# A stable log-sum-exp: the first load split into two rows and fourteen

## The chip, the core and the metric

The kernel runs on one core of one Trainium2 chip. The metric is the device time of one execution in microseconds, the median of the runs shown. One further execution is recorded by the hardware profiler; all durations of single instructions and packets come from that one.

## The reference

For each of 32 x 512 rows of 1,024 float32 numbers, drawn from a normal distribution, one number is wanted:

```python
max_x = np.max(x, axis=-1, keepdims=True)
return max_x.squeeze(-1) + np.log(np.sum(np.exp(x - max_x), axis=-1))
```

That is 16,384 rows, or 67.1 MB to read and 65.5 KB to write.

## The kernel before

The kernel computes log(sum(exp(x))) without the maximum, and checks at the end that every sum lies between 1e-15 and 1e15; only if one does not, a branch computes everything again with the maximum. With these inputs the branch is not taken.

The 16,384 rows are spread over 128 partitions, 128 rows to each. The first 112 rows of each partition (`W`) are one contiguous piece of the input, the other 16 (`B`) another. Below, "a row" means one row in every partition: 128 x 4 KB, or 512 KB.

The table `LOADS` is the whole plan. Each entry is one DMA: its size in rows, and what is done with the rows that it completes. Loads shrink from 16 rows to less than one. All are issued by SP, in the order of the table, on one queue (`load`, line 127). Each has its own semaphore (`landed[i]`), and ACT waits for it (`act.wait(landed[i], 16)`).

All loads go into `ring`, a buffer of 48 rows in each partition. The first 48 rows fill it once; a later load has to wait until the reductions that read its place are done. `users` holds who last used which part, and `load` makes SP wait for every user that overlaps the new load.

ACT takes the exponential of every row in place (line 212). The row sums are then made in one of several ways, which the letter in the table names:

- `R16`: one DVE `reduce_sum` over 16 rows (line 223).
- `F9`: POOL adds the upper half of each row to the lower one (line 217), and DVE sums the halves (line 159).
- `T3`: DVE adds the halves and sums the result in one instruction for each row (line 232).
- `Y` and `Z`: the last row, in two pieces; ACT sums while it takes the exponential (line 190).

For a group of a kind, ACT issues one instruction for all its rows, and so does DVE for `R`.

The order of the work on each engine is the order in which the function emits it; no scheduler moves anything, with one exception. The first load is taken out of its place when the program is finalised, and is put on SP's list ahead of the barrier at which all engines meet at the start (`start_early`):

```python
first_load = first_load or dma.ins
...
first = here.instructions.pop(k)
...
top.insert(k, first)
```

The second and all later loads are issued behind that barrier.

At the end ACT takes the logarithm of the sums in three pieces (lines 251, 262 and 264), SP stores them with two DMAs (lines 259 and 268), and PE and DVE work out whether all sums were in range (lines 134 to 148, 274 to 283).

Of the kernel before, what the change touches and what calls it, by code (L numbers as in the profile page):

```python
# [15 lines left out]


LOADS = [
    (16, "R16"), (16, "R16"), (16, "R16"), (16, "F9 R7"), (13.5, "F6 R7"), (12.5, "R7 F6"),
    (9, "R5 F4"), (7.5, "F4 R3"), (5.5, "F4 R2"), (4.59375, "T4"), (3.25, "T3"), (2.5, "T3"),  # L20
    (1.78125, "T2"), (1.25, "T1"), (0.9375, "T1"), (0.6875, "T1"), (0.53125, "Y"), (0.46875, "Z"),
]
# [372 lines left out]
```

## Time and profile before

| What | Value |
|---|---|
| median of three runs | 162.02 us (161.79 to 163.18) |
| profiled execution | 161.82 us |
| its span, first to last instruction | 160.5 us |
| ACT busy | 114.5 us (71%) |
| DVE busy | 113.8 us (71%) |
| POOL busy | 37.2 us (23%) |
| DMA, mean over the span | 419 GB/s |
| first load issued | 0.00 us |
| second load issued | 1.44 us |
| first exponential starts | 21.92 us |
| last exponential starts | 158.02 us |

Times in the profile count from the span's start, which is the issue of the first load. "Busy" does not count time in which an instruction waits for a semaphore. In the timeline each row gives the start, the time taken, the engine, the line, the operation, output and input, the number of instructions merged into the row, and in brackets how long the engine had been idle before and what ended that. "SPq" rows are the issues of DMAs by SP, not the transfers.

### The profile page before, as it was taken

How to read it: one execution, taken by the hardware profiler on the slowest of the kernel's cores; microseconds unless marked ns; L12 is line 12 of the kernel's file. 1: busy time of each engine (PE TensorE's matmuls, PEld its weight loads, DVE VectorE, ACT ScalarE, POOL GpSimd, SP SyncE). 2: the span in 40 equal slices, each digit the busy share in tenths (PEclk: the TensorE clock that was granted, in tenths of full speed). 3: DMA queues.
4: the chain of work that ended last, by engine and by line, in shares of the span. 5: the costliest groups of instructions: out<-in, count | busy, mean ns of one | idle time of the engine just before them, and what ended most of it. 6: DMA issues, size and time to landing. Idle time of an engine off the chain costs nothing.

```text
span 160.5 us, 208 instructions
## 1 busy us (share of the span) xinstructions
PE 2.1 (1%) x24; PEld 1.0 (1%) x24; DVE 113.8 (71%) x53; ACT 114.5 (71%) x30; POOL 37.2 (23%) x10
## 2 busy tenths in 40 slices
PE   0000000000000000000000000000000000000022
PEld 0000000000000000000000000000000000000011
DVE  0000000009999499994999859959999999999995
ACT  3000059990799708995099949992999979989996
POOL 0000000000000000000000993690004969873000
DMA  8996996996996996996999999999999999999992
GB/s 278 506 523 278 506 523 261 523 523 261 523 523 261 523 506 278 523 490 294 482 441 441 441 425 408 408 408 498 423 423 404 406 426 421 449 406 427 417 407 80
DMA packets 2880, 67.18 MB, mean 419 GB/s; under 512 B 576, under 2 KB 704, under 8 KB 1344
## 3 DMA queue, kind: packets, MB, share of 16 engines
q1 hardware_dynamic: 2880, 67.18, 97.7%
HBM read 67.11 MB, written 0.07 MB: 419 GB/s over the span
## 4 chain that ended last, share of the span: by engine, by line
DMA 55%; DVE 22%; ACT 20%; SPq 0%; issue 0%; PE 0%; DVEq 0%
DMA ring<-in_x_dram 55%; ACT ring L212 20%; DVE sumexp L223 15%; DVE ring L232 4%; DVE sumexp L159 2%; SPq L127 0%; DVE clamped L139 0%; DVE clamped L134 0%; PE count L148 0%; PE count L280 0%; DVE clamped L274 0%; DVE fine L283 0%; DVEq L44 0%
## 5 line engine op out<-in xcount | busy, mean ns | idle before, releaser
L212 ACT ACTIVATE ring<-ring 128x16384 f32<-128x16384 f32 (+16 forms) x22 | 111.6, 5121 | 43.1 <-DMA ring<-in_x_dram 43.1
L223 DVE TENSOR_REDUCE sumexp<-ring 128x16 f32<-128x16384 f32 (+4 forms) x9 | 85.6, 9514 | 43.1 <-ACT ring L212 43.1
L217 POOL TENSOR_TENSOR ring<-ring 128x2048 f32<-128x2048 f32 (+2 forms) x6 | 37.0, 6171 | 108.5 <-ACT ring L212 108.5
L159 DVE TENSOR_REDUCE sumexp<-ring 128x4 f32<-128x2048 f32 (+2 forms) x6 | 18.4, 3078 | 0.1
L232 DVE SCALAR_TENSOR_TENSOR ring<-ring 128x512 f32<-128x512 f32 x15 | 9.5, 687 | 0.0
L115 ACT ACT_TABLE_LOAD x1 | 1.3, 1283 | 1.4 <-PEq L57 1.4
L144 PE MATMUL count<-far,bad 128*1 128x1 f32 x2 | 0.2, 164 | 153.3 <-DVE clamped L139 153.3
L148 PE MATMUL count<-sumexp,ones 128*1 128x1 f32 x20 | 1.8, 164 | 3.5 <-DVE ring L232 3.4
L232 DVE DVE_READ_ACCUMULATOR ring<-ring 128x1 f32 x15 | 1.2, 83 | 0.0
L190 ACT ACTIVATE last_exp<-ring 128x544 f32<-128x544 f32 (+1 forms) x2 | 1.2, 578 | 0.0
L116 DVE MEMSET ones<- 128x1 f32 x1 | 0.1, 59 | 1.5 <-PEq L57 1.5
L144 PEld LDWEIGHTS count<-far,bad 128*1 128x1 f32 x2 | 0.1, 82 | 153.3 <-DVE clamped L139 153.3
L148 PEld LDWEIGHTS count<-sumexp,ones 128*1 128x1 f32 x20 | 0.8, 81 | 4.4 <-DVE ring L232 4.3
L283 DVE TENSOR_SCALAR fine<-count 1x1 int32<-1x1 f32 x1 | 0.1, 145 | 0.5 <-PE count L148 0.5
L190 ACT ACTIVATION_READ_ACCUMULATOR last_exp<-ring 128x1 f32 x2 | 0.4, 186 | 0.0
L139 DVE SCALAR_TENSOR_TENSOR clamped<-clamped,sumexp 128x119 f32<-128x119 f32 x1 | 0.3, 283 | 0.0
L264 ACT ACTIVATE res<-sumexp 128x1 f32<-128x1 f32 x1 | 0.3, 294 | 0.0
L251 ACT ACTIVATE res<-sumexp 128x112 f32<-128x112 f32 x1 | 0.3, 280 | 0.0
L134 DVE TENSOR_SCALAR clamped<-sumexp 128x119 f32<-128x119 f32 x1 | 0.2, 223 | 0.0
L274 DVE SCALAR_TENSOR_TENSOR clamped<-sumexp 128x9 f32<-128x9 f32 x1 | 0.2, 169 | 0.1
L262 ACT ACTIVATE res<-sumexp 128x15 f32<-128x15 f32 x1 | 0.2, 198 | 0.0
L280 PE MATMUL count<-far,bad 128*1 128x1 f32 x2 | 0.2, 164 | 0.0
(8 smaller groups left out, 0.7 us busy)
## 6 DMA issues: line engine op xcount, KB each, us to landing
ring<-in_x_dram SPq DMA_DIRECT2D x1, 6912.0 KB, 23.9
ring<-in_x_dram SPq DMA_DIRECT2D x1, 6400.0 KB, 19.7
ring<-in_x_dram SPq DMA_DIRECT2D x1, 4608.0 KB, 15.9
ring<-in_x_dram SPq DMA_DIRECT2D x1, 3840.0 KB, 12.4
ring<-in_x_dram SPq DMA_DIRECT2D x1, 2816.0 KB, 18.7
ring<-in_x_dram SPq DMA_DIRECT2D x1, 2352.0 KB, 23.8
ring<-in_x_dram SPq DMA_DIRECT2D x1, 1664.0 KB, 21.1
ring<-in_x_dram SPq DMA_DIRECT2D x1, 1280.0 KB, 23.7
```

The costliest lines, as they stand in the source:

```text
L115: nc.scalar.preload_act_table_set("natural_log_exp_and_others")
L139: dve.did(nc.vector.scalar_tensor_tensor(out=clamped[:, 0:LATE], in0=clamped[:, 0:LATE], scalar=0.0, in1=sumexp[:, 0:LATE], op0=ALU.bypass ...
L144: pe.did(nc.tensor.matmul(count, lhsT=bad[:, 0:1], rhs=far, start=True, stop=False))
L148: return pe.did(nc.tensor.matmul(count, lhsT=ones, rhs=sumexp[:, c : c + 1], **kw))
L159: at = dve.did(nc.vector.reduce_sum(out=sumexp[:, c0 : c0 + s0], in_=halves, axis=AX.X))
L190: at = act.did(nc.scalar.activation(out=last_exp[:, here - p : end - p], in_=ring[:, here:end], func=AF.Exp, accum_out=sumexp[:, LAST : NC ...
L212: at = act.did(nc.scalar.activation(out=v, in_=v, func=AF.Exp))
L217: at = pool.did(nc.gpsimd.tensor_tensor(out=rows[:, :, 0:H], in0=rows[:, :, 0:H], in1=rows[:, :, H:d], op=ALU.add))
L223: who = (dve, dve.did(nc.vector.reduce_sum(out=sumexp[:, c : c + s], in_=rows, axis=AX.X)))
L232: who = (dve, dve.did(nc.vector.scalar_tensor_tensor(out=lo, in0=lo, scalar=1.0, in1=rows[:, r, H:d], op0=ALU.mult, op1=ALU.add, accum_out ...
L251: ln_early = act.did(nc.scalar.activation(out=res[:, 0:W], in_=sumexp[:, 0:W], func=AF.Ln))
L264: ln_last = act.did(nc.scalar.activation(out=res[:, LAST:NC], in_=sumexp[:, NC : NC + 1], func=AF.Ln, bias=sumexp[:, LAST:NC]))
```

## The change

The first entry of the table becomes two. The first load brings two rows, the second fourteen, and each has an exponential and a reduction of its own size. Sizes, places in the ring and work of all other rows stay as they are.

```diff
@@ -16,7 +16,7 @@
 LOADS = [
-    (16, "R16"), (16, "R16"), (16, "R16"), (16, "F9 R7"), (13.5, "F6 R7"), (12.5, "R7 F6"),
+    (2, "R2"), (14, "R14"), (16, "R16"), (16, "R16"), (16, "F9 R7"), (13.5, "F6 R7"), (12.5, "R7 F6"),
     (9, "R5 F4"), (7.5, "F4 R3"), (5.5, "F4 R2"), (4.59375, "T4"), (3.25, "T3"), (2.5, "T3"),
     (1.78125, "T2"), (1.25, "T1"), (0.9375, "T1"), (0.6875, "T1"), (0.53125, "Y"), (0.46875, "Z"),
 ]
```

The load that is issued ahead of the start barrier is always the first of the table. In the changed kernel that is the one of two rows; the fourteen rows follow as the first DMA behind the barrier. There is one more load, with one more semaphore, one more exponential on ACT and one more reduction on DVE. The order of everything else on each engine is the same.

## The prediction

> **What bounds the kernel now.** I read the page's busy shares first, then the chain, then the timeline of the first 80 us, then a table by stage. Part 1, the DMA rows of parts 2 and 3, and the chain:
>
> ```profile
> PE 2.1 (1%) x24; PEld 1.0 (1%) x24; DVE 113.8 (71%) x53; ACT 114.5 (71%) x30; POOL 37.2 (23%) x10
> ...
> GB/s 278 506 523 278 506 523 261 523 523 261 523 523 261 523 506 278 523 490 294 482 441 441 441 425 408 408 408 498 423 423 404 406 426 421 449 406 427 417 407 80
> ...
> q1 hardware_dynamic: 2880, 67.18, 97.7%
> ...
> DMA 55%; DVE 22%; ACT 20%; SPq 0%; issue 0%; PE 0%; DVEq 0%
> ```
>
> No compute engine is over 71%, and the one load queue is at 97.7%. The chain's 20% of ACT and 22% of DVE do not mean that they hold the stream up: the chain steps through a reduction because its end lets a load be issued, but the stages say that this load then waits in line anyway. The timeline shows it:
>
> ```profile
> 0.00 53.38 SPq L127 DMA_DIRECT2D ring<-in_x_dram  x4
> ...
> 21.92 13.86 ACT L212 ACTIVATE ring<-ring 128x16384 f32<-128x16384 f32 x1 [19.19 <-DMA ring<-in_x_dram]
> 35.81 17.22 DVE L223 TENSOR_REDUCE sumexp<-ring 128x16 f32<-128x16384 f32 x1 [34.20 <-ACT ring L212]
> 41.24 13.86 ACT L212 ACTIVATE ring<-ring 128x16384 f32<-128x16384 f32 x1 [5.46 <-DMA ring<-in_x_dram]
> ...
> 60.59 13.86 ACT L212 ACTIVATE ring<-ring 128x16384 f32<-128x16384 f32 x1 [5.49 <-DMA ring<-in_x_dram]
> ...
> 79.94 13.95 ACT L212 ACTIVATE ring<-ring 128x9216 f32<-128x9216 f32 x2 [5.50 <-DMA ring<-in_x_dram]
> ```
>
> ACT starts when a load lands: at 21.92, 41.24, 60.59 and 79.94, one 16-row load every 19.34 us (1.209 us a row), with 5.5 us of idle time each. The fourth load waits for the first reduction (35.81 + 17.22 = 53.03) and is issued by 53.38; the third lands only at 60.59, so the fourth is over 7 us early. By stage, between landings (columns: busy time of PE, PEld, DVE, ACT and POOL, then the TensorE clock, the DMA share and GB/s):
>
> ```profile
> 21.92:41.24 19.32, 0.00 (x0) 0.00 (x0) 5.43 (x1) 13.86 (x2) 0.00 (x0) 1.00 1.00 434
> 41.24:60.60 19.36, 0.00 (x0) 0.00 (x0) 17.26 (x2) 13.87 (x2) 0.00 (x0) 1.00 1.00 433
> ...
> 143.70:150.80 7.10, 0.00 (x0) 0.00 (x0) 6.99 (x12) 7.08 (x3) 2.24 (x1) 1.00 0.99 421
> 150.80:157.40 6.60, 1.32 (x14) 0.60 (x14) 6.53 (x22) 6.60 (x7) 0.00 (x0) 1.00 0.99 398
> ```
>
> The DMA share is 0.99 to 1.00, from the first stage to the last. (The saw in the GB/s row is how 2.4 us packets fall into 4 us slices; 278, 506 and 523 average 436.) From 143.7 on ACT is full too, in step with the stream:
>
> ```profile
> 143.72 6.99 ACT L212 ACTIVATE ring<-ring 128x4704 f32<-128x4704 f32 x2 [0.60 <-DMA ring<-in_x_dram]
> ```
>
> It idled 0.60 us just before, until a load landed. So no compute time saved or lost in the first 60 us reaches the end; only a shift of the stream does. The time is start of the stream, 128 rows at 1.209 us (155 us), and a tail of some 3 us.
>
> **The change, part by part.**
>
> *Exponential and sum of the first load.* One ACT instruction becomes two and one DVE reduction becomes two. The 128x2048 exponential is a row of before: 1.89 us; the 128x2048 reduction: 2.28 us. The 14-row ones are 13.86 - 2 x 0.87 = 12.1 us and 17.22 x 14/16 = 15.1 us. ACT was idle 19.19 us and DVE 34.20 us before their first work, so the two-row pieces lie wholly in idle time. The 14-row chain ends at about 22 + 12.1 + 15.1 = 49.2 instead of 53.03. That lets the next 16-row load be issued about 3.8 us earlier, behind one that still has 11 us to run: worth 0. If the idle time were not there, the extra instructions would cost 0.3 us on ACT (1.89 + 12.1 - 13.86, rounded up); nothing is late next, as the DMA queue is what everything waits for.
>
> *Waits.* The issue that reuses the first ring slots now waits for two reductions, not one; both are DVE counts and the later one decides. Behind it on SP are only later load issues, which have their own ring waits. Cost 0 with 7 us of cover.
>
> *The two loads in the stream.* The trace's packet records give the price of smaller packets. A load is 128 packets, eight to each of the 16 DMA engines. 65,536-byte packets take 2.418 us each, 10,240-byte ones 0.385, 7,296-byte ones 0.276. The line between the last two gives 0.309 us for the 8,192 bytes of a two-row load; eight are 2.47 us, against 2.42 for the same bytes in one 65,536-byte packet. The 14-row packets (57,344 bytes) lie next to the 13.5-row ones (2.041 us for 55,296): 2.117 us, eight are 16.93, as against 16.93 for seven large ones. Sum +0.06 us.
>
> *One more load boundary.* Steps between landings equal the packets alone: 19.34 us is 8 x 2.418. A boundary between queued loads costs 0.
>
> *The hand-over from the first load to the second.* This is the one place that before does not show: only the first load is issued ahead of the start-up barrier. The second is issued behind it:
>
> ```profile
> 1.44 0.33 SPq L127 DMA_DIRECT2D ring<-in_x_dram  x1
> ```
>
> Before, that issue is covered by the first load's 20 us of transfer. After, the cover is two rows. When do they end? By the packet records the first packets start at 1.01 to 1.69 us and end at 3.95 to 4.64, engine by engine. One such packet holds as many bytes as eight 8,192-byte ones, so the two-row load leaves each engine at about 4.0 to 4.7 us. When is the second ready? The first load needs 1.01 to 1.69 us from issue to first packet; from 1.44 that is 2.45 to 3.13. Margin: 0.8 us or more for the earliest engine. I take 0. Upper bound: nothing overlaps, and a whole start and landing are exposed: 1.01 us to the first packet, 0.4 to 1.05 us by which first packets exceed 2.418 us, and 0.34 us from the first load's last packet (21.56) to its landing: 1.8 to 2.4 us. Lower bound: the slow first packets owe their 0.4 to 1.05 us to their size, and small ones save most of it: -1 us. Zero is nearest to the landings' steps.
>
> The Trainium skill (DMA: Bandwidth & Descriptors, "Anatomy of one DMA — SWDGE (gpsimd) path") speaks against this edit: its fit charges every DMA a fixed 2.0 us beside its bytes, which taken serially would give an estimated 164.0 us. The even landings of this trace disagree for queued loads, and the page itself puts most of the 2 us into the completion rather than the setup.
>
> **Sum.** Profiled execution 161.82 us (span 160.5 and 1.3 around it) + 0.06 = 161.9. The runs shown have a median of 162.02, 0.2 above the profiled one, and spread from 161.79 to 163.18; on that scale the forecast is **162.1 us**, no change.
>
> **Rivals.**
>
> *A hole at the hand-over (slower).* The place is the DMA queue at 4 us. It decides when the barrier releases SP more than 0.8 us later than the 1.44 us of this profile, in executions without a profiler for instance, or when the second load needs more than 2.5 us from issue to packets. Each us beyond that is lost whole, since the stream never catches up. For: nothing else is queued there. Against: SP needs only 1.44 us through the barrier here, and the run times agree with the profiled one. A partial hole of 0.3 to 1.5 us gives 162.4 to 163.6; the whole start exposed, 163.9 to 164.5. The skill's fixed charge is the second of these.
>
> *A cheaper start (slightly faster).* Small first packets save part of the 0.4 to 1.05 us: 161.0 to 161.7. Against: that excess looks like a latency before the first bytes, which a small packet meets as well.
>
> *The change frees the ring earlier and so moves the stream (what an early start might be for).* The price would be the holes that it fills; the stages show a DMA share of 1.00 there, so 162.1 again.
>
> **How the numbers follow.** Forecast, with the third rival: 0.82. Partial hole: 0.09, of which 0.04 beyond 1%. Whole start exposed: 0.04. Cheaper start: 0.05, of which 0.02 beyond 1% (on top of the spread of the runs). A measurement of this kernel, whose runs spread by 0.9%, tells about 1% (1.6 us) from no change. Faster 0.02, same 0.90, slower 0.08. The range runs from 161.4 (part of a cheaper start) to 163.2 (the top of the runs of before, and most partial holes).
>
> **What the profile after would show.** Two-row landing (first exponential) near 5.1 us; the 14-row exponential at 21.9 to 22.1 and then landings at 41.3, 60.7 and 80.0, each within 0.2 of before; a DMA share near 1 between 4 and 8 us; the last exponentials within 0.2 us of 157.38; the load issue that stands at 53.05 in before at about 49. A 14-row exponential after 22.3 us would show a hole, of the size of the delay, and every later landing would be late by the same. The prediction is wrong if the landings keep their places and the time still moves, since then something beside the stream sets it.

## The result and the profile after

The changed kernel takes 164.40 us (median; 163.99 to 164.69) against 161.96 (161.78 to 163.41) for the kernel before in the same series: 1.0144 times as long, 95% interval 1.0119 to 1.0169. The forecast of 162.1 us and its range up to 163.2 were too low. Repeated on another occasion it took 163.75 against 161.88, 1.0104 times (1.0087 to 1.0121). By the medians the loss is 1.9 to 2.4 us.

From the page of the changed kernel, the busy shares, the DMA throughput, the load queue and the chain:

```profile
PE 2.1 (1%) x24; PEld 1.0 (1%) x24; DVE 113.9 (70%) x54; ACT 114.7 (70%) x31; POOL 37.2 (23%) x10
...
GB/s 341 365 449 449 435 512 273 514 497 353 433 497 433 353 514 417 353 514 481 357 460 433 433 395 464 414 414 415 433 382 376 444 393 433 404 411 423 417 344 19
...
q1 hardware_dynamic: 3024, 67.18, 96.6%
...
DMA 55%; DVE 22%; ACT 20%; SPq 1%; issue 0%; PE 0%; DVEq 0%
```

Compute has hardly changed: ACT is busy 0.2 us longer, DVE 0.1 us. The span is 2.9 us longer (163.4 against 160.5), and the share of the load queue fell from 97.7% to 96.6%. The time went into the stream. The timeline says where. Each ACT row whose bracket names the DMA begins where a load has landed; the number in the bracket is how long the engine had been idle. First the start of the changed kernel:

```profile
4.66 1.91 ACT L212 ACTIVATE ring<-ring 128x2048 f32<-128x2048 f32 x1 [1.93 <-DMA ring<-in_x_dram]
...
22.98 12.15 ACT L212 ACTIVATE ring<-ring 128x14336 f32<-128x14336 f32 x1 [16.41 <-DMA ring<-in_x_dram]
35.16 15.09 DVE L223 TENSOR_REDUCE sumexp<-ring 128x14 f32<-128x14336 f32 x1 [26.27 <-ACT ring L212]
42.33 13.86 ACT L212 ACTIVATE ring<-ring 128x16384 f32<-128x16384 f32 x1 [7.20 <-DMA ring<-in_x_dram]
...
61.68 13.86 ACT L212 ACTIVATE ring<-ring 128x16384 f32<-128x16384 f32 x1 [5.50 <-DMA ring<-in_x_dram]
```

The first sixteen rows are complete at 22.98 instead of 21.92: **1.06 us late**. The next two landings are late by 1.09 each, so the steps between them are those of before. Then the later part, first of before and then of after (before goes on at 143.72, as shown above):

```profile
111.41 18.90 ACT L212 ACTIVATE ring<-ring 128x6656 f32<-128x6656 f32 x4 [3.31 <-DMA ring<-in_x_dram]
131.44 11.69 ACT L212 ACTIVATE ring<-ring 128x4096 f32<-128x4096 f32 x4 [1.13 <-DMA ring<-in_x_dram]
```

```profile
112.50 18.90 ACT L212 ACTIVATE ring<-ring 128x6656 f32<-128x6656 f32 x4 [3.31 <-DMA ring<-in_x_dram]
134.12 11.65 ACT L212 ACTIVATE ring<-ring 128x4096 f32<-128x4096 f32 x4 [2.73 <-DMA ring<-in_x_dram]
146.58 4.12 ACT L212 ACTIVATE ring<-ring 128x4704 f32<-128x4704 f32 x1 [0.80 <-DMA ring<-in_x_dram]
```

At 112.50 the kernel is still 1.09 us late. At 134.12, where the load of 7.5 rows has landed, it is 2.68 late: **another 1.6 us** was lost in one load, far from the change. That load's row among the DMA issues (size, time from issue to landing), of before and then of after:

```profile
ring<-in_x_dram SPq DMA_DIRECT2D x1, 3840.0 KB, 12.4
```

```profile
ring<-in_x_dram SPq DMA_DIRECT2D x1, 3840.0 KB, 14.0
```

So there are two losses: one where the second load takes over from the first, which was a rival of the prediction, and one that no part of the prediction names.

The packet records of the trace (start, duration and size of every packet) show the first. They don't name the DMA engine, but while an engine has work its next packet begins within 4 ns of the end of the one before, so its packets can be followed. The two-row load leaves the 16 DMA engines between 3.9 and 4.3 us; the forecast was 4.0 to 4.7. The second load was issued when it should be:

```profile
1.44 0.33 SPq L127 DMA_DIRECT2D ring<-in_x_dram  x1
```

But its first packets start between 3.89 and 4.85 us, the last of them 3.4 us after the issue began. Some engines go on without a pause; three stand still for at least 0.5 us and at most 0.94, and the first packets take 2.2 to 3.0 us instead of 2.12. In the load of 7.5 rows the same two signs are seen at 121.7 to 124 us: pauses of 0.6 us and more on four of the sixteen engines, and packets of 1.5 to 2.3 us instead of 1.14 on those four and a fifth. A load counts as landed when its last engine is done, so the slowest engine decides. In that load the spread between the first and the last engine's landing grows from 1.19 to 2.59 us.

### The profile page after: what moved, and what is told of

The parts are those of the page before. It is cut to its first block, busy times and chain, and to the rows that moved or that the text cites. A ratio compares the mean times of both kernels' runs of the same rounds, so it can differ in the third digit from the quotient of the medians.

```text
span 163.4 us, 212 instructions
## 1 busy us (share of the span) xinstructions
PE 2.1 (1%) x24; PEld 1.0 (1%) x24; DVE 113.9 (70%) x54; ACT 114.7 (70%) x31; POOL 37.2 (23%) x10
## 3 DMA queue, kind: packets, MB, share of 16 engines
q1 hardware_dynamic: 3024, 67.18, 96.6%
## 4 chain that ended last, share of the span: by engine, by line
DMA 55%; DVE 22%; ACT 20%; SPq 1%; issue 0%; PE 0%; DVEq 0%
DMA ring<-in_x_dram 55%; ACT ring L212 20%; DVE sumexp L223 15%; DVE ring L232 4%; DVE sumexp L159 2%; SPq L127 1%; DVE clamped L139 0%; DVE clamped L134 0%; PE count L148 0%; PE count L280 0%; DVE clamped L274 0%; DVE fine L283 0%; DVEq L44 0%
## 5 line engine op out<-in xcount | busy, mean ns | idle before, releaser
L212 ACT ACTIVATE ring<-ring 128x2048 f32<-128x2048 f32 (+17 forms) x23 | 111.7, 4907 | 45.8 <-DMA ring<-in_x_dram 45.8
L223 DVE TENSOR_REDUCE sumexp<-ring 128x7 f32<-128x7168 f32 (+5 forms) x10 | 85.8, 8578 | 45.6 <-ACT ring L212 45.6
```

What stands on the lines that cost most here:

```text
L212: at = act.did(nc.scalar.activation(out=v, in_=v, func=AF.Exp))
L223: who = (dve, dve.did(nc.vector.reduce_sum(out=sumexp[:, c : c + s], in_=rows, axis=AX.X)))
```

## The experiments

Each time is a median, and the kernel before ran beside it in the same series: 161.88 us for the first four runs, 161.93 for the next four, 161.81 for the last four. "Late" below is measured at the landing, against the profile of before.

### Where the second load takes over

`e1_after_again` is the changed kernel unaltered.

> The changed kernel (2 rows, then 14) once more, for a second trace. In its first trace the 14-row landing came 1.08 us later than in before, and a second loss of about 1.6 us showed at 123 us, in the load of 7.5 rows, on all DMA engines. Theory A (a hole where the second load takes over, plus an unrelated disturbance in that one execution): the 14-row exponential again at 22.6 to 23.1, the later loss absent, so 163.0 to 163.2. Theory B (the small first load puts the stream into a state that costs at several places): both losses again, 164.2 to 164.7.

163.75 us, below the 164.2 to 164.7 of theory B and above the 163.0 to 163.2 of theory A; the traced execution took 164.47. Its ACT:

```profile
22.65 12.15 ACT L212 ACTIVATE ring<-ring 128x14336 f32<-128x14336 f32 x1 [15.85 <-DMA ring<-in_x_dram]
...
134.02 11.67 ACT L212 ACTIVATE ring<-ring 128x4096 f32<-128x4096 f32 x4 [2.94 <-DMA ring<-in_x_dram]
```

The 14-row exponential starts 0.73 late, and the 7.5-row load lands 2.58 us late, so both losses are there again. The second is no accident of one execution, and theory A falls. Of theory B, a loss at several places is there; that a small first load causes it is tested below. (The expectation puts the later loss of the first trace on all DMA engines; its packets show it on the five named above.)

`e2_both_early` issues both parts of the split ahead of the barrier:

```diff
-        first_load = first_load or dma.ins
+        if i < 2:
+            first_loads.append(dma.ins)
...
+        for load_ins in first_loads:
...
+            top.insert(k, first)
```

> Two rows, then 14, but both loads are issued ahead of the start barrier (the second at about 0.4 us instead of 1.44). If the loss is the second load's late issue, its packets are ready before the first load's are done, the 14-row exponential starts at 21.9 to 22.2, and the time is 161.9 to 162.3. If any second load early on costs, however early it is issued (its own slow first packets), the 14-row exponential stays at 22.6 to 23.1 and the time at 163.8 to 164.7.

162.36 against 161.88, 1.0024 times (1.0006 to 1.0042), just above the first of the two ranges. The timeline of its ACT:

```profile
21.68 12.15 ACT L213 ACTIVATE ring<-ring 128x14336 f32<-128x14336 f32 x1 [14.99 <-DMA ring<-in_x_dram]
...
131.93 11.70 ACT L213 ACTIVATE ring<-ring 128x4096 f32<-128x4096 f32 x4 [1.82 <-DMA ring<-in_x_dram]
```

The first sixteen rows are there at 21.68, even 0.24 us before those of the kernel before: with the second load issued 1 us earlier (0.44 instead of 1.44) the first loss is gone. Small packets at the start cost nothing here. The second loss is still there, if smaller: 0.49 late at 131.93, after being 0.2 early until then.

`e3_4_12` gives the second load twice the cover (the lines are those of the changed kernel and of this run):

```diff
-    (2, "R2"), (14, "R14"), (16, "R16"),
+    (4, "R4"), (12, "R12"), (16, "R16"),
```

> Four rows, then 12, the second load behind the barrier as in the changed kernel. The cover is 4.8 us of transfer instead of 2.4, so the first load ends at about 6.4 to 7.1 us. Late issue: no hole, the 12-row exponential at 21.9 to 22.2, 161.9 to 162.3 us. A cost of each extra load early on: 163.8 to 164.7 as with 2 and 14.

163.61 us, 1.009 times (1.0063 to 1.0118), in neither range but nearer to the one for a cost of each extra load. For the start the trace says otherwise:

```profile
22.10 10.44 ACT L212 ACTIVATE ring<-ring 128x12288 f32<-128x12288 f32 x1 [10.90 <-DMA ring<-in_x_dram]
...
133.29 11.69 ACT L212 ACTIVATE ring<-ring 128x4096 f32<-128x4096 f32 x4 [2.75 <-DMA ring<-in_x_dram]
```

The landing at 22.10 is 0.18 late, without a pause between the loads. Two rows more of cover take the first loss away as well as an earlier issue does. Nearly all that is lost is lost at the 7.5-row load (1.85 late at 133.29).

`e4_14_2` swaps the two:

```diff
-    (2, "R2"), (14, "R14"), (16, "R16"),
+    (14, "R14"), (2, "R2"), (16, "R16"),
```

> Fourteen rows, then two: as many loads as the changed kernel, but the first one covers 17 us. Late issue: no hole at all, 161.9 to 162.3 us. If one more load in the list is what costs (a longer queue, one more semaphore, a small load among large ones): 163.8 to 164.7.

163.23 us, 1.0084 times (1.0067 to 1.0101): my expectation for the late issue failed, since it left the second loss out. There is no pause at the take-over. The sixteen rows land at 22.43, 0.53 late, because one engine's very first packet took 1.5 us longer than its bytes need (at most 1.05 in before). The other 0.9 us is lost at the 7.5-row load. So the second loss does not need a small first load; all four kernels that have it carry a nineteenth load.

### The later loss

What the four kernels share is that the 7.5-row load is the ninth DMA of the queue and not the eighth. Before it stand 72 packets on each engine instead of 63 (eight of data and one that counts the semaphore, for each load). The next four runs test that with DMAs that carry next to nothing.

`e5_before_1tiny` and `e6_before_2tiny` are the kernel before with one or two of them, behind the third load (the buffer, its semaphore and a wait for it at the very end are left out here):

```diff
+        if i == 2:
+            for e in range(1):
+                nc.sync.dma_start(out=idle[:, 16 * e : 16 * e + 16], in_=x_rows[:, 16 * e : 16 * e + 16]).then_inc(extra, 16)
```

> The kernel before with its 16-row first load, and one tiny DMA more (64 bytes to each partition, into a buffer that nothing reads) issued behind the third load. Every later load is then one place further back in the queue's count, with the data stream and the start unchanged. In all four kernels with 19 loads, the load of 7.5 rows, there the ninth DMA, lost 0.7 to 1.6 us on some DMA engines; in before it is the eighth and loses nothing. Theory C (the place in the count decides): that load starts late or slowly on some engines, and the time is 162.6 to 163.4. Theory D (the loss needs a split first load, through engines that are out of step): no such loss, 161.9 to 162.1.

163.09 against 161.93, 1.0074 times (1.005 to 1.0097), in the range of theory C. With the first load whole, at the old place and on time, 8 KB of data that nobody reads cost 1.2 us:

```profile
21.83 13.86 ACT L217 ACTIVATE ring<-ring 128x16384 f32<-128x16384 f32 x1 [19.10 <-DMA ring<-in_x_dram]
...
132.90 11.67 ACT L217 ACTIVATE ring<-ring 128x4096 f32<-128x4096 f32 x4 [2.59 <-DMA ring<-in_x_dram]
```

The stream is on time until the 7.5-row load, and 1.46 late there. Theory D falls, and with it the small first load of theory B.

> The kernel before with two tiny DMAs behind the third load. The load of 7.5 rows is then the tenth DMA, and the 9-row load the ninth; that one is issued 4 us or more ahead of its turn, against 2.1 to 2.8 us for the load of 7.5 rows. Theory C in its narrow form (the ninth DMA's packets come late, and only cover decides): no loss, 161.9 to 162.2. If any place from the ninth on costs: 162.6 to 163.4. Theory D: 161.9 to 162.2.

162.76 us, 1.0041 times (1.0015 to 1.0067); in its trace the same load loses 1.3 us as the tenth DMA. The narrow form, that only the ninth is slow, falls too.

`e7_after_1tiny` and `e8_both_early_1tiny` add one tiny DMA to the changed kernel and to the one with both early.

> The changed kernel (2 rows, then 14) with one tiny DMA behind its fourth load, so that the load of 7.5 rows is the tenth DMA. Theory C, narrow: the loss at the hand-over at 4 us stays (the 14-row landing 0.7 to 1.1 us late), the later loss goes, 162.6 to 163.0. Theory D: both stay, 163.5 to 164.5.

163.98 us, 1.0128 times (1.009 to 1.0165): above the 162.6 to 163.0 of theory C in its narrow form. In the trace (an execution of 163.32, the fastest of four) the 7.5-row load still loses 0.3 us; the first loss stays, and there the last engine starts the 14 rows only 4.0 us after their issue.

> Two rows and 14, both issued ahead of the start barrier, and one tiny DMA behind the fourth load. Theory C, narrow: neither loss is left, and as its 14-row landing came 0.2 us earlier than in before, 161.6 to 161.9. Theory D: as without the tiny DMA, 162.4.

163.18 us, 1.0072 times (1.0056 to 1.0089), with 1.3 us lost at the 7.5-row load. That is above both ranges. It agrees with no form of the count in which a tenth place would be safe: in all nine traces in which at least 72 packets stand before it on each engine, that load loses time.

`e11_before_1part` sends the tiny DMA to one partition, so that one engine at most has another data packet (the line of `e5_before_1tiny` and that of this run, both cut short at "..."):

```diff
-                nc.sync.dma_start(out=idle[:, 16 * e : 16 * e + 16], ...
+                nc.sync.dma_start(out=idle[0:1, 16 * e : 16 * e + 16], ...
```

> The kernel before with a tiny DMA behind the third load that goes to one partition only, so that one DMA engine at most carries a packet of it. If the number of DMAs in the queue decides, several engines start the 7.5-row load slowly, as with the tiny DMA to 128 partitions: 162.8 to 163.4. If the number of packets on each engine decides, only one engine is late (which still sets the landing) or none: 161.9 to 163.0.

161.97 us, 1.0025 times (1.0003 to 1.0047). In its trace the 7.5-row load is on time:

```profile
131.38 11.70 ACT L217 ACTIVATE ring<-ring 128x4096 f32<-128x4096 f32 x4 [1.13 <-DMA ring<-in_x_dram]
```

The slowest of its 128 packets takes 1.26 us instead of 1.14. The engine that carried the tiny DMA had 65 packets before this load (63, one of data and one for the semaphore); it went on without a pause and took 1.14 us for each. That speaks for the packets that stand on each engine, not for the number of DMAs. It does not settle it: the trace is of one of the fastest executions (161.81 us), and of twelve executions four took 162.6 to 163.6, against one of 29 (162.69) of the kernel before in the same series. Of those four there is no trace, so the number of DMAs, or a loss on one engine alone, may still count.

### More cover for the load that starts late

Why is it this load? It needs half a row of the ring that the 13.5-row load's half sums still hold, so SP issues it only when that reduction ends: 2.1 to 2.8 us before the engines finish the load ahead of it in before, 1.6 to 2.8 in after. Its issue, in before and then in after:

```profile
119.04 0.33 SPq L127 DMA_DIRECT2D ring<-in_x_dram  x1
```

```profile
120.13 0.33 SPq L127 DMA_DIRECT2D ring<-in_x_dram  x1
```

Apart from the second load of a split start no other has so little; next comes the 12.5-row load, 3.4 us ahead in before and 2.8 in after, whose trace shows one slow packet there that delays no landing. A load of 7 rows needs no such half row and goes out right behind the 9-row load. `e9_after_7_6`, `e10_both_early_7_6` and `e12_before_7_6` make this edit in the changed kernel, in the one with both early and in the kernel before:

```diff
-    (9, "R5 F4"), (7.5, "F4 R3"), (5.5, "F4 R2"),
+    (9, "R5 F4"), (7, "F4 R3"), (6, "F4 R2"),
```

> The changed kernel (2 rows, then 14), with the loads of 7.5 and 5.5 rows made 7 and 6. The 7.5-row load had to wait for the half row of the ring behind its seven, and came only 1.6 to 2.8 us ahead of its turn; a 7-row load needs no wait of its own and is issued right behind the 9-row one, some 15 us ahead, and the 6-row load some 10 us ahead. Theory C2 (from the ninth DMA on, a load that is issued under 3 us ahead of its turn starts late on some engines): the later loss goes and that of the hand-over stays, 162.6 to 163.2. If the later loss has another cause: 163.5 to 164.5 as before.

162.86 against 161.81, 1.0052 times (1.0037 to 1.0066), as theory C2 had it. The issue of the 7-row load, and ACT:

```profile
107.79 0.43 SPq L127 DMA_DIRECT2D ring<-in_x_dram  x1
```

```profile
22.88 12.15 ACT L212 ACTIVATE ring<-ring 128x14336 f32<-128x14336 f32 x1 [15.98 <-DMA ring<-in_x_dram]
...
112.40 18.89 ACT L212 ACTIVATE ring<-ring 128x6656 f32<-128x6656 f32 x4 [3.32 <-DMA ring<-in_x_dram]
131.83 6.27 ACT L212 ACTIVATE ring<-ring 128x4096 f32<-128x4096 f32 x2 [0.54 <-DMA ring<-in_x_dram]
```

0.96 late at 22.88, 0.99 late at 112.40, and between 119 and 139 us no packet is more than 0.02 us slower than others of its size: with 14 to 15 us of cover the second loss is gone, and what is left of the time, 1.05 us, is the first.

> Two rows and 14, both issued ahead of the barrier, and loads of 7 and 6 rows. Theory C2: neither loss, and the 14-row landing 0.2 us earlier than the 16-row one of before: 161.5 to 161.9. Otherwise 162.0 to 163.0.

161.77 us, 0.9988 times (0.9978 to 0.9999), in the range of theory C2. Neither loss:

```profile
21.87 12.15 ACT L213 ACTIVATE ring<-ring 128x14336 f32<-128x14336 f32 x1 [15.03 <-DMA ring<-in_x_dram]
...
130.85 6.27 ACT L213 ACTIVATE ring<-ring 128x4096 f32<-128x4096 f32 x2 [0.54 <-DMA ring<-in_x_dram]
```

The split is then worth what the prediction said of it, nothing: 0.04 us under the kernel before, 0.12 under the control. The 0.24 us that the start had gained in the first kernel of this kind is 0.05 here.

> The kernel before with loads of 7 and 6 rows in place of 7.5 and 5.5, the control for the two above. The eighth load lost nothing before, so nothing is to be won: 161.7 to 162.0.

161.89 us, 1.0002 times (0.9994 to 1.0011). The eighth load had nothing to lose.

The later loss in all traces with the 7.5-row load. "Step" is the time from the last engine's landing of the 9-row load to that of the 7.5-row load; "spread" is from the first engine's landing to the last one's.

| kernel | place | packets before it, each engine | step, us | spread before, after, us |
|---|---|---|---|---|
| before | 8 | 63 | 9.11 | 0.62, 0.61 |
| before, tiny DMA to one partition | 9 | 63 (one engine 65) | 9.11 | 0.54, 0.53 |
| 2 and 14 | 9 | 72 | 10.71 | 1.19, 2.59 |
| 2 and 14, again | 9 | 72 | 10.92 | 0.76, 2.38 |
| both early | 9 | 72 | 9.79 | 0.28, 0.95 |
| 4 and 12 | 9 | 72 | 10.73 | 0.63, 2.11 |
| 14 and 2 | 9 | 72 | 10.01 | 0.90, 1.80 |
| before, one tiny DMA | 9 | 72 | 10.56 | 0.38, 1.71 |
| before, two tiny DMAs | 10 | 81 | 10.41 | 0.45, 1.63 |
| 2 and 14, one tiny DMA | 10 | 81 | 9.42 | 0.98, 1.29 |
| both early, one tiny DMA | 10 | 81 | 10.44 | 0.41, 1.65 |

## Why the prediction was wrong

**What bounds the kernel: right.** ACT and DVE have the busy times that were worked out (12.15 and 15.09 us for the 14-row pieces, against 12.1 and 15.1), and none of it reaches the end. Every us lost is lost in the stream and never caught up, as the hole's rival said. Two readings on the way were not right, and nothing hangs on them. The DMA share of the stages that the prediction leaves out runs from 0.95 to 1.01, since a packet is counted whole where it starts (the stretch from 1.0 to 1.4 us, in which most first packets start, reads 7.15); the even steps between landings carry the point. And 1.89 + 12.1 - 13.86 is 0.13 us, not 0.3; ACT was busy 0.2 us longer.

**The price of smaller packets: right.** 8,192-byte packets take 0.309 us, as interpolated, and 57,344-byte ones 2.116 (2.117). The two rows landed at 4.64, by the last engine, and not near 5.1: in this trace small first packets lost less at the start than large ones.

**The hand-over: wrong, and the first of the two steps that failed.** The cover was sized nearly right (the engines are free at 3.9 to 4.3 us). The readiness was not: "the first load needs 1.01 to 1.69 us from issue to first packet" was carried over to a second load, and the second needs up to 3.4 us (1.44 to 4.85) while the first one's packets are moving and two more loads are issued behind it. The margin of 0.8 us was not there. An issue 1 us earlier or a cover twice as long removes the loss (`e2_both_early`, `e3_4_12`), so the margin is shown to be its cause. The first load started on an idle queue, so its row was no measure; which part of a busy start holds the second load up, the moving packets or the issues behind it, was not tested. The rival had the place, the mechanism and almost the threshold (2.5 us), and its partial form (162.4 to 163.6) holds the 162.86 us that this loss gives by itself; its chance of 0.09 was far too small for a step that the trace of before did not show. That the rival's full form (163.9 to 164.5) holds the measured 164.40, and that the estimate of 164.0 us from a fixed charge for each DMA comes near it (by the title of its section a charge of the gpsimd path, while SP issues the loads here), is luck: the hand-over cost 1.06 us, and the rest was lost elsewhere. The Trainium skill (DMA: Bandwidth & Descriptors, "Latency and other measured facts") puts the first byte of a DMA issued by SP at about 0.6 us. On the idle queue of before, the first packet comes 1.01 us after the issue begins and about 0.6 after it ends (it takes 0.39 us), which agrees if the end is meant; the last engine's comes 1.69 us after the beginning, and on the busy queue of after it took up to 3.4.

**Waits and the extra boundary: wrong, and the second step.** "Cost 0 with 7 us of cover" was right for the load that the sentence was about. But the split puts every later load one place back in the queue, and their cover was not gone through. The 7.5-row load had only 2.1 to 2.8 us of it, visible in before as an issue at 119.04 and a landing of the load ahead at 122.3 (its last packets end some 0.4 us before that). That was enough in the trace of before, at the eighth place, and not at the ninth: 0.3 to 1.8 us lost in the traces of the split kernels with this load, 1.6 us in that of the changed kernel. In the traces both conditions are needed: one tiny DMA brings the loss into the kernel before, whose start and cover are unchanged (`e5_before_1tiny`), and more cover takes it out of the changed kernel with the ninth place kept (`e9_after_7_6`). "A boundary between queued loads costs 0" held within 0.2 us at all other boundaries.

**The sum.** 1.06 us at the hand-over, 1.6 at the 7.5-row load and 0.2 of small drifts make the 2.9 us by which the span grew.

**Still open.** Why a load with little cover starts late on some engines from the ninth place on. The traces exclude a small first load (one tiny DMA does it), engines out of step (the spread before it was 0.28 to 1.19 us, without order) and, so far as one trace tells, the number of DMAs alone. 63 packets on each engine were harmless in the trace, 65 on one engine too, and 72 were not; whether there is a limit between them, and of what kind, was not tried. Nor is the eighth place proven safe: of 69 executions of the kernel before six took 162.6 us or more (up to 163.41), and none of those was traced.

## What to carry to other kernels

Where a stream of loads is the bound, list for every load how long before its turn it is issued, not only for those that the edit touches; here the loads that lost time had 1.6 to 3.2 us, engine by engine, and loads with 3.4 us or more on every engine lost none. One more DMA, far ahead, was enough to tip such a load. The time from issue to first packet on an idle queue was no measure for a load that is issued while others move. A load that waits for a sliver of a buffer can be cut at the border of what is free: half a row less gave 14 to 15 us of cover here.

## What the runs showed of the hardware that was not expected

- The second load, issued by SP 1.44 us after the first, took 3.4 to 4.0 us until its packets moved on all 16 engines (the four traces with 2 rows first and 14 behind the barrier); the first load, on an idle queue, took 1.01 to 1.81 in the traces in which its packets were large.
- The delay differs from engine to engine, from none to between 0.5 and 0.94 us of standing still in the changed kernel, and it is not made up: a spread of 1.19 us at the second landing was still 1.19 at the eighth, 100 us later.
- One tiny DMA, 64 bytes to each of 128 partitions, behind the third load cost 1.2 us (163.09 against 161.93). It ran at about 60 us, and the loss came some 60 us later, at the 7.5-row load with its 2.4 to 2.8 us of cover.
